# Forty-eight adaLN modulation tiles as row products on VectorE instead of matmuls on TensorE, in the first mixer of a two-layer backbone

## Chip, cores and metric

One core of one Trainium2 chip runs the whole program. The metric is the device time of one execution in microseconds (us), the median of three runs. Engines are called TensorE (PE, its weight loads PEld), VectorE (DVE), ScalarE (ACT), GpSimd (POOL) and SyncE (SP, whose queue issues nearly all DMAs).

## What is computed

Two layers over 256 context and 256 latent tokens of width 1024. Each layer has a token mixer with four branches (gated linear attention, Hyena convolution, HGRN2, differential attention), merged by gates and projected, and then a mixture of 16 experts. Both halves are modulated by vectors that come from the conditioning vectors `c` (latents) and `c_ctx` (context):

```
sc, scc = silu(c), silu(c_ctx)
for l in range(DEPTH):
    mod_x = split(sc  @ ada_w[l] + ada_b[l], 6)
    mod_c = split(scc @ ada_w[l] + ada_b[l], 6)
    h  = rms_norm(x) * (1 + mod[1]) + mod[0]
    x  = x + mod[2] * mixer(h)
    h2 = rms_norm(x) * (1 + mod[4]) + mod[3]
    x  = x + mod[5] * experts(h2)
```

`ada_w[l]` is 1024 x 6144 in float32, so one of its six chunks is 4 MB. Only two vectors are multiplied with it, so nearly all of the work is bringing it in.

## The kernel before

The tokens lie along the free dimension, the 1024 channels over 128 partitions in 8 blocks. `mixer(l, ...)` goes through the blocks of the input projection one by one. `load(name)` brings a block of weights (128 x 1024, 512 KB) by a DMA on SP, ScalarE rounds it to a high part (L798), and VectorE forms the low part by a subtraction (L799). `col_block` then runs 24 matmuls of 512 columns over 8 blocks of channels (high times high, high times low, low times high) into the PSUM tile `pd`. Around these blocks stand: the filters of the Hyena branch for both layers (`hyena_filters`, L692 to L730), the scan of the gated linear attention (`scan`, L878 to L977, tiles `ps`), two HGRN2 units with a scan each (`hg_unit`), the norms and rotations of the attention's q and k (`group_rsqrt` L654, L1144 to L1152), the attention, and `merge`, which takes 8 blocks of gates for each of the four branches (L852, L860, L864). The Hyena branch itself runs between the second and the third merge.

The modulation of layer 0 for chunks 2 to 5 and of layer 1 for chunks 1 and 0, 48 tiles of 512 KB in all, runs in the background of the first mixer. `AdaBack.run(n)` is called with a credit after each level of a scan, each query block, each block of weights. A step (`Ada.step`, L466) brings a tile of 128 rows and 1024 columns of `ada_w` into one of two buffers and runs four matmuls with 32 stationary columns (two of them are the vectors) into the PSUM tile `pa`, each on its own 32 columns of the array. After the eighth tile of a chunk, `mod_write` copies the sum (L446), transposes it on TensorE (L425, tile `pm`), and adds the bias into `mod[l]` (L453, twice). Layer 1's chunks 2 to 5 come later, at the end of the first experts, in the same way.

The order in which instructions stand on each engine is not that of the code. A scheduler gives each instruction a priority by its place in the code, and lets an engine take work from further on when nothing earlier is ready by its own reckoning. The engines then run their queues strictly in order. The numbers behind a tile's name in order listings count tiles; `base` is the large SBUF area, `r` with a number one of the areas that change type with the phase.

Of the kernel before, what the change touches and what calls it, by code (L numbers as in the profile page):

```python
# [13 lines left out]
AF = mybir.ActivationFunctionType  # L14
# [3 lines left out]
D = 1024  # L18
# [5 lines left out]
RA, RB = 12288, 12288                            # columns of the two regions that change type with the phase  # L24
BASE = 52736 - RA - RB
ENGS = ('AV', 'AVG')                             # engines of the copies of q and k, by layer
# steps of the modulation (by layer, of which parts may be left over) among the other work
TR = (0, 2, 0.5)                                 # at the end of the experts, before and among the second mixer's h
SCN = (0.5, 0.5)                                 # per level of a scan
FL = (1, 1)                                      # the rest before the merge  # L30
DAS = (0.5, 1)                                   # per head and query block
ADA = (2, 2)                                     # per block of w_in
FIRST = ("gk", "gq")                             # blocks of the second mixer loaded during the experts
AHEAD = ((0, 0), (0, 5))                         # tiles of experts loaded during the mixers


# ---------------------------------------------------------------- layouts
# [21 lines left out]
LATE = CN.at["adab"][0]                          # those from here on give way to weights of the experts  # L59
C0 = Pack()                                      # needed at the start only  # L60
# [104 lines left out]
def dft():  # L165
    """Transforms at the odd frequencies 2 pi (k + 1/2) / 512, k < 256, where no wrapped term meets the 511 of the
    convolution. Phases are counted from the middles of the signal, 127.5, of the filter's tap 128, and of the
    outputs 128..383; cosines are then even and sines odd in t <-> 255 - t, and half of the t will do."""
# [10 lines left out]
def pack_inputs(a):  # L179
    """Layout of the inputs; every element is a copy of an input's element or a constant of the shapes."""  # L180
# [50 lines left out]
    for l in range(2):  # L231
# [5 lines left out]
        wb = a["w_branch"][l].reshape(4, 2, 128, 2, 4, 128)          # i, k, p, half, d, n  # L237
        for i in range(4):
            for h in range(2):
                wg[l, BIDX[f"wb{i}{h}"]] = wb[i, :, :, h].transpose(1, 2, 0, 3).reshape(128, 8, 128)   # p, (d, k), n  # L240
# [4 lines left out]
    o["wa"] = wa.reshape(2, 128, KB * 32)  # L245
    for n in ("ada_w", "moe_w1", "moe_w3", "moe_w2"):
        o[n] = np.ascontiguousarray(a[n])
# [3 lines left out]
# ---------------------------------------------------------------- device  # L251
class Mem:
    """Columns of one SBUF tile, those longest free first; Tile sees which bytes each instruction touches."""
# [7 lines left out]
    def take(self, n, avoid=None):  # L261
        """avoid: first and last + 1 of columns not to be touched."""
# [39 lines left out]
    def merge(self):  # L302
        """Joins neighbouring free runs (their stamps become the latest)."""
        out = []
        for o, c, t in self.free:
            if out and out[-1][0] + out[-1][1] == o:
                o0, c0, t0 = out.pop()
                o, c, t = o0, c0 + c, max(t, t0)
            out.append((o, c, t))
        self.free = out  # L310

    def cut(self, b, n):
        """Gives the first n columns of b back; the rest stays."""
# [12 lines left out]
class Buf:  # L326
# [3 lines left out]
    def __call__(self, off=0, dims=None, p0=0, np_=128, n=None):  # L330
        """AP of rows p0..p0+np_, from column off, free dims [[stride, count], ...]."""
# [19 lines left out]
def build(tc, ins, outT, dbg=None, stop=None):  # L351
# [30 lines left out]
    # ---------------- persistent  # L382
    cn = mem.take(CN.n)
    sm = mem.take(SM.n)                              # of the layer
    cs_b = mem.take(256)
    mod = [mem.take(96) for _ in range(2)]          # [6 chunk, 8 k, 2 stream]
    xb = [mem.take(4096), 0]                         # [stream, k, 256]; columns cut off in front
    x_at = xb[0].at
    NR = 3
    raws = [mem.take(1024) for _ in range(NR)]       # blocks of the mixers' weights as they come  # L390
# [45 lines left out]
    # ---------------- adaLN  # L436
    def load_c(c):
        """silu(c) of both streams, 32 columns for each block of 128."""
# [17 lines left out]
    class Ada:  # L456
        """Streams ada_w[l] in tiles of one k-block of a 1024-column chunk."""
# [17 lines left out]
    class AdaBack:  # L475
        """The same in the background, in two buffers of its own."""
# [6 lines left out]
        def run(self, n=None):  # L483
            """n: steps, or parts of one."""
# [12 lines left out]
    # ---------------- little helpers  # L497
    def rsqrt_small(x, n, y, t):
        """y = x ** -0.5 on n columns (x, y, t: functions of nothing giving APs)."""
# [6 lines left out]
    def rms_rows(l, t0, mem=mem, nsq=3):  # L506
        """1/rms over d of x, on every partition: PSUM [128, 512 - t0]."""
# [26 lines left out]
    class TokenSums:  # L534
        """Sums over d while x comes block by block: x^2, and x against a [d, 16] matrix per stream."""
# [17 lines left out]
        def tokens(self, mem):  # L553
            """PSUM [token, [tb, s] of x^2 | 64: [tb, s, 16]]."""
# [17 lines left out]
    def rs_tokens(p, ns, mem):  # L572
        """1/rms: Buf whose columns 8.. are [tb, s]."""
# [6 lines left out]
    def bcast_rs(s, ns):  # L580
        """PSUM [128, (s, t)]: 1/rms on every partition."""
# [157 lines left out]
    def mixer(l, last, ada_bg, rm, sums):  # L739
# [518 lines left out]
        if FL[l]:  # L1258
            ada_bg.run()
# [506 lines left out]
```

## Time and profile before

| | before |
|---|---|
| median of 3 runs | 2050.81 us (2050.77 to 2059.14) |
| span of the profiled execution | 2046.6 us, 4.2 us under the median |
| PE busy | 1883.5 us, 92% |
| DVE busy | 801.6 us, 39% |
| ACT busy | 525.8 us, 26% |
| HBM read | 544.03 MB, 267 GB/s over the span |

The span runs from the first to the last instruction of the one execution that the profiler took; the runs' times include what lies around it. A matmul's end is modelled, so a busy PE is one that has matmuls under way. In the trace a float32 matmul stands as two records, so the four matmuls of a modulation tile are eight records.

### The profile page before, as it was taken

The numbers are of one execution on the slowest core, as the hardware profiler recorded it, in microseconds if no ns is written. First come the engines' busy times: TensorE is split into PE (matmuls) and PEld (weight loads), VectorE is DVE, ScalarE is ACT, GpSimd is POOL, SyncE is SP. The second block draws the span as 40 slices with busy tenths as digits, with TensorE's granted clock in tenths as the row PEclk, the third lists the DMA queues.
The fourth block names the chain that finished last, engine by engine and source line by source line (L and its number), as shares of the span: only waits on it lengthen the run. The fifth ranks groups of instructions, "written<-read, shape, count | busy, mean of one in ns | idle before, by whom it ended". The sixth has DMA issues, their size and how long they took to land.

```text
span 2046.6 us, 28476 instructions
## 1 busy us (share of the span) xinstructions
PE 1883.5 (92%) x11722; PEld 1091.5 (53%) x11722; DVE 801.6 (39%) x1768; ACT 525.8 (26%) x929; POOL 27.4 (1%) x52
## 2 busy tenths in 40 slices
PE   7999999999999799999887899999998999997877
PEld 3666677887886434434232356888996433231213
DVE  5455648747442323212120245769864111010101
ACT  4433336622231211101000243447442100000000
POOL 0000000000000000000000010001000000000000
PEclk9989999999999899999999999999999999999999
DMA  7734521222335799999999855324577999999999
GB/s 306 231 128 145 185 95 63 93 92 74 134 121 219 293 388 386 351 409 409 409 409 409 320 201 194 106 95 143 196 257 287 388 409 409 409 409 409 409 409 331
DMA packets 154005, 549.03 MB, mean 268 GB/s; under 512 B 11026, under 2 KB 22674, under 8 KB 153108
## 3 DMA queue, kind: packets, MB, share of 16 engines
q1 hardware_dynamic: 153300, 544.08, 70.3%
q0 software_dynamic: 576, 3.15, 0.4%
q8 instruction: 92, 1.51, 0.3%
q14 instruction: 37, 0.30, 0.0%
HBM read 544.03 MB, written 3.15 MB: 267 GB/s over the span
## 4 chain that ended last, share of the span: by engine, by line
PE 72%; DMA 18%; DVE 5%; issue 3%; ACT 2%; SPq 0%; DVEq 0%; ACTq 0%
PE pd L428 42%; PE ps L428 15%; DMA r<-moe_w 8%; PE pm L428 7%; DMA base<-moe_w 6%; PE pa L428 6%; DMA base<-ada_w 2%; PE pm L425 2%; DMA base<-wg 1%; PE ps L1591 1%; ACT r L798 1%; DVE r L799 1%; DMA base<-xT 0%; PE ps L425 0%; DVE r L1189 0%
## 5 line engine op out<-in xcount | busy, mean ns | idle before, releaser
L428 PE MATMUL pd<-r 128*128 128x256 f32 (+3 forms) x2976 | 582.8, 365 | 11.2 <-DMA r<-moe_w 6.7
L428 PEld LDWEIGHTS pd<-r 128*128 128x128 f32 (+2 forms) x2976 | 424.9, 184 | 146.1 <-issue 73.1
L428 PE MATMUL pd<-r,r 128*128 128x512 f32 (+3 forms) x1304 | 282.5, 433 | 12.1 <-DMA r<-moe_w 9.4
L799 DVE TENSOR_TENSOR r<-base,r 128x1024 fp32r<-128x1024 f32 x136 | 165.8, 1221 | 159.7 <-ACT r L798 156.5
L428 PEld LDWEIGHTS pd<-r,r 128*128 128x128 f32 (+2 forms) x1304 | 161.8, 166 | 107.0 <-issue 58.3
L798 ACT ACTIVATE r<-base 128x1024 fp32r<-128x1024 f32 x136 | 143.3, 1058 | 283.1 <-PE pd L428 224.2
L428 PE MATMUL ps<-base 32*64 32x64 f32 (+12 forms) x2372 | 176.7, 278 | 13.2 <-DMA base<-hy 4.8
L428 PE MATMUL pd<-r,base 128*32 128x512 f32 (+1 forms) x680 | 167.8, 599 | 13.5 <-DMA r<-moe_w 11.5
L428 PEld LDWEIGHTS ps<-base 32*64 32x64 f32 (+7 forms) x2372 | 112.4, 142 | 74.2 <-issue 42.2
L428 PE MATMUL pm<-base 128*128 128x128 f32 (+12 forms) x660 | 112.8, 327 | 18.9 <-issue 11.6
L428 PE MATMUL ps<-r,base 128*64 128x512 f32 (+4 forms) x468 | 98.6, 525 | 13.5 <-DVE base L1592 6.3
L428 PEld LDWEIGHTS pm<-base 128*128 128x128 f32 (+5 forms) x660 | 73.8, 180 | 66.1 <-issue 38.6
L428 PE MATMUL pd<-base 128*32 128x512 f32 (+1 forms) x408 | 101.4, 596 | 6.4 <-DMA base<-moe_w 5.6
L428 PEld LDWEIGHTS pd<-r,base 128*32 128x32 f32 (+1 forms) x680 | 42.0, 122 | 113.7 <-issue 74.4
L1588 DVE TENSOR_TENSOR r<-base,pd 64x512 f32<-64x512 f32 x16 | 10.9, 680 | 212.6 <-PE pd L428 212.6
L1587 ACT ACTIVATE base<-pd 128x512 f32<-128x512 f32 (+1 forms) x32 | 19.0, 594 | 253.9 <-PE pd L428 253.9
L1588 DVE TENSOR_TENSOR base<-base,pd 128x512 f32<-128x512 f32 x16 | 11.0, 687 | 185.7 <-PE pd L428 151.5
L428 PE MATMUL pa<-r,r 128*128 128x512 f32 (+1 forms) x384 | 82.6, 342 | 1.1 <-DVE base L860 1.1
L428 PE MATMUL pa<-base 128*32 128x256 f32 (+1 forms) x704 | 74.6, 399 | 7.7 <-DMA base<-ada_w 7.5
L428 PE MATMUL pd<-base,r 128*32 128x512 f32 (+1 forms) x296 | 71.3, 597 | 9.4 <-DMA base<-moe_w 9.4
L1638 ACT ACTIVATE base<-ps 32x512 f32<-32x512 f32 (+2 forms) x28 | 14.7, 525 | 253.8 <-PE ps L428 249.4
L1638 ACT ACTIVATE r<-ps 32x512 f32<-32x512 f32 (+2 forms) x32 | 15.3, 479 | 247.6 <-PE ps L428 242.1
(241 smaller groups left out, 1636.2 us busy)
## 6 DMA issues: line engine op xcount, KB each, us to landing
r<-moe_w SPq DMA_DIRECT2D x251, 1024.0 KB, 18.1
base<-moe_w SPq DMA_DIRECT2D x131, 1024.0 KB, 17.7
base<-wg SPq DMA_DIRECT2D x152, 512.0 KB, 3.3
base<-ada_w SPq DMA_DIRECT2D x84, 512.0 KB, 4.6
r<-ada_w SPq DMA_DIRECT2D x12, 512.0 KB, 10.7
base<-xT SPq DMA_DIRECT2D x4, 1024.0 KB, 6.5
filters<-r SPq DMA_DIRECT2D x8, 256.0 KB, 4.0
base<-filters POOLq DMA_DIRECT2D x2, 1024.0 KB, 6.6
```

The lines of the kernel that those rows point to most:

```text
L425: T.transpose(out, in_, ident)
L428: return T.matmul(out, lhsT, rhs, start=start, stop=stop, **kw)
L798: A.activation(w[0](), raw(), AF.Copy)
L799: V.tensor_tensor(w[1](), raw(), F(w[0]()), op=OP.subtract)
L1587: A.activation(s_(np_=rows), pa[0:rows, :], AF.Silu)
L1588: V.tensor_tensor(h_(np_=rows), s_(np_=rows), pb[0:rows, :], op=OP.mult)
L1591: T.transpose(p[:, q * rows:q * rows + rows], h_(q * 128, n=128, np_=rows), cs("ident", n=rows, np_=rows))
L1638: A.activation(dst, src, AF.Copy)
```

## The change

The inputs get two more arrays: `ada_t`, `ada_w` with the columns of a chunk's 128-column block as rows (a block is 128 x 1024, contiguous), and `cb`, the two conditioning vectors. A class `AdaRows` takes the place of `AdaBack` in the first mixer. At its start it brings `cb` to all 128 partitions and applies SiLU in one ScalarE instruction. A step brings one block of `ada_t` into one of two buffers, and for each of the two vectors runs one `tensor_tensor_reduce` on VectorE: product of the block with the vector, sum along the row, started at the bias, into one column of `mod[l]`. The products themselves go to a scratch tile, or for the second vector over the block. Credits in layer 0 are now given only once `merging` is set: 1.25 for each block of weights, the rest before the output projection. The matmuls, `mod_write` and the PSUM tile `pa` of these 48 tiles fall away. The second layer's modulation stays as it was, and so do the first 16 tiles.

```diff
-SCN = (0.5, 0.5)
-FL = (1, 1)
-DAS = (0.5, 1)
-ADA = (2, 2)
+SCN = (0, 0.5)
+FL = (0, 1)
+DAS = (0, 1)
+ADA = (0, 2)
+ADM = (1.25, 2)
...
+    o["ada_t"] = np.ascontiguousarray(a["ada_w"].reshape(2, D, 48, 128).transpose(0, 2, 3, 1))
+    o["cb"] = np.stack([a["c_ctx"], a["c"][0]])
...
+    class AdaRows:
+        def __init__(self, todo):
+            self.todo = [(l, c, j) for l, c in todo for j in range(8)]
+            self.buf = mem.take(5120)
+            self.raw, self.junk, self.cb = [view(self.buf, 1024 * i, 1024) for i in range(2)], view(self.buf, 2048, 1024), view(self.buf, 3072, 2048)
+            src = ins["cb"]
+            S.dma_start(out=self.cb(n=2048), in_=bass.AP(tensor=src.tensor, offset=src.offset, ap=[[0, 128], [1, 2048]]))
+            A.activation(self.cb(n=2048), self.cb(n=2048), AF.Silu)
+            self.left, self.credit, self.n = len(self.todo), 0, 0
+
+        def run(self, n=None):
+            self.credit = self.left if n is None else self.credit + n
+            while self.credit >= 1 and self.left:
+                l, c, j = self.todo.pop(0)
+                b = self.raw[self.n % 2]
+                S.dma_start(out=b(), in_=ins["ada_t"][l, c * 8 + j])
+                for s in range(2):
+                    V.tensor_tensor_reduce(self.junk() if s == 0 else b(), b(), self.cb(s * 1024, n=1024), 1.0,
+                                           cs("adab", l * 48 + c * 8 + j, n=1), OP.mult, OP.add,
+                                           mod[l](c * 16 + j * 2 + s, n=1))
+                self.n += 1
+                self.left -= 1
+                self.credit -= 1
+                if not self.left:
+                    self.buf.free()
...
-            ada_bg.run(ADA[l])
+            ada_bg.run((ADM if merging[0] else ADA)[l])
...
-                p = ps("s" if ada_bg.left else "a")
+                p = ps("s" if l and ada_bg.left else "a")
...
+        merging[0] = True
         merge(0, True)
         merge(2, False)
-        ada_bg.run()
+        if l:
+            ada_bg.run()
...
         merge(3, False)
         merge(1, False)
+        ada_bg.run()
...
-                ada = AdaBack([(0, c) for c in range(2, 6)] + [(1, 1), (1, 0)], mem.take(2048))
+                ada = AdaRows([(0, c) for c in range(2, 6)] + [(1, 1), (1, 0)])
```

Lines of the changed program lie about 31 further down in the mixer: L799 becomes L830, L917 L948, L935 to L939 L966 to L970, L860 L891, L654 L685, L1144 L1175. The product stands in listings as `L519 ISA`, two instructions: the product over 1024 columns, and the reading of its sum, 128x1.

On VectorE, at the filters of layer 1's Hyena branch (L723 to L731 now), the order before has the chain of small steps alone:

```order
79 L692 TENSOR_SCALAR r_530<-ps_604,base 64x256
80 L799 TENSOR_TENSOR r_227<-base,r_227 128x1024
81 L693 TENSOR_SCALAR r_530<-r_530 64x256
82 L694 TENSOR_SCALAR r_530<-r_530 64x256
83 L699 SCALAR_TENSOR_TENSOR r_530<-r_530 64x256 x3
84 L700 TENSOR_SCALAR r_530<-r_530 64x256
85 L692 TENSOR_SCALAR r_530<-ps_614,base 64x256
```

The same place in the changed program:

```order
104 L730 SCALAR_TENSOR_TENSOR r_485<-r_485 64x256
105 L519 ISA base<-base 128x1024
106 L519 ISA base 128x1
107 L730 SCALAR_TENSOR_TENSOR r_485<-r_485 64x256
108 L519 ISA base<-base 128x1024
109 L519 ISA base 128x1
110 L730 SCALAR_TENSOR_TENSOR r_485<-r_485 64x256
```

The products now stand between the links of the chain. They are not in the merge: the first of the 96 is row 67 of VectorE's order, the last row 511, and the first gate step of a merge (L891) is row 533. Ten stand before the chain above, 35 from there to the end of the first scan, 38 in the two HGRN2 units, 13 in the norms and rotations of the attention's q and k.

On TensorE, in the first scan (the 64x64 matmuls on tiles `ps`), the order before puts blocks of weights (`pd`) and modulation tiles (`pa`, 32x256) between the heads:

```order
99 L428 MATMUL ps_771<-base 64x64 x8
100 L428 MATMUL ps_781<-base 64x64 x8
101 L428 MATMUL ps_791<-base 64x64 x8
102 L428 MATMUL ps_801<-base 64x64 x8
103 L428 MATMUL pa_1231<-base 32x256 x3
104 L428 MATMUL pd_1241<-r_227 128x512 x8
105 L428 MATMUL ps_815<-base 64x64 x8
```

Now 31 such tiles of the scan follow each other with nothing between them; these are the last of them:

```order
85 L431 MATMUL ps_932<-base 64x64 x8
86 L431 MATMUL ps_947<-base 64x64 x8
87 L431 MATMUL ps_958<-base 64x64 x8
88 L431 MATMUL ps_969<-base 64x64 x8
89 L431 MATMUL pd_1138<-r_227 128x512 x3
90 L431 MATMUL ps_980<-base 64x64 x8
91 L431 MATMUL pd_1138<-r_227 128x512 x14
```

Of the 52 block matmuls that stood among those of the first scan, 17 now come at its very end and some 28 after it, between the first scan and the second.

## Rows read from the trace of the kernel before

**Rows 1.** The page: engines, and the chain that ended last by engine.
```profile
PE 1883.5 (92%) x11722; PEld 1091.5 (53%) x11722; DVE 801.6 (39%) x1768; ACT 525.8 (26%) x929; POOL 27.4 (1%) x52
PE 72%; DMA 18%; DVE 5%; issue 3%; ACT 2%; SPq 0%; DVEq 0%; ACTq 0%
```

**Rows 2.** Stretches: length, then PE, PEld, DVE, ACT, POOL busy, PEclk, DMA share, GB/s.
```profile
55.40:87.30 31.90, 31.65 (x216) 23.15 (x217) 9.47 (x17) 20.25 (x27) 0.31 (x1) 1.00 0.69 232
87.30:161.20 73.90, 69.80 (x834) 47.37 (x828) 42.30 (x88) 22.86 (x40) 2.17 (x4) 0.91 0.47 151
161.20:294.60 133.40, 130.20 (x1290) 92.90 (x1290) 63.50 (x127) 43.95 (x79) 3.44 (x5) 1.00 0.43 144
294.60:318.40 23.80, 22.68 (x107) 17.27 (x108) 19.70 (x51) 11.86 (x17) 0.00 (x0) 1.00 0.27 90
400.00:680.00 280.00, 279.64 (x1218) 210.51 (x1217) 131.38 (x192) 75.55 (x103) 0.00 (x0) 1.00 0.36 129
```

**Rows 3.** Timeline: start, duration, engine, line; a modulation tile on PE and its neighbours.
```profile
91.32 0.64 PE L428 MATMUL pa<-base 128*32 128x256 f32 x8 [0.20 <-DMA base<-ada_w]
91.89 2.14 PE L428 MATMUL pd<-r,r 128*128 128x512 f32 x8
```

**Rows 4.** Waits from 60 to 320 us: who for what, us, times, longest.
```profile
PEld pa L428 <- DMA base<-ada_w: 8.7, 11, 1.7
PE pa L428 <- DMA base<-ada_w: 5.0, 6, 1.5
```

**Rows 5.** Timeline of VectorE: two 128x1024 products of two tensors, one step between.
```profile
52.72 1.22 DVE L799 TENSOR_TENSOR r<-base,r 128x1024 fp32r<-128x1024 f32 x1
53.85 0.41 DVE L778 TENSOR_TENSOR r<-base,r 128x256 fp32r<-128x256 f32 x1
54.19 1.22 DVE L799 TENSOR_TENSOR r<-base,r 128x1024 fp32r<-128x1024 f32 x1
```

**Rows 6.** VectorE's groups by shape, 0 to 700 us: count, busy us, mean ns, idle.
```profile
L1204 DVE TENSOR_SCALAR base<-base 128x1 f32<-128x1 f32 x32 | 4.2, 145 | 0.1
L1210 DVE SCALAR_TENSOR_TENSOR base<-base 128x512 f32<-128x512 f32 x8 | 6.0, 746 | 0.1
L446 DVE COPY base<-pa 128x256 f32<-128x256 f32 x8 | 3.4, 419 | 4.6 <-PE pa L428 4.5
L453 DVE TENSOR_TENSOR base<-pm,base 128x8 f32<-128x8 f32 x16 | 2.0, 157 | 0.6 <-PE pm L425 0.5
```

**Rows 7.** Timeline of VectorE: one level of the first scan and the next one's start.
```profile
139.44 1.68 DVE L917 COPY_PREDICATED base<-base,ps 128x256 f32<-128x256 int32 x4
141.02 0.67 DVE L937 TENSOR_TENSOR base<-base 128x512 f32<-128x512 f32 x1
141.73 0.19 DVE L939 TENSOR_TENSOR base<-base 128x32 f32<-128x32 f32 x1
142.02 0.69 DVE L935 TENSOR_TENSOR base<-base 128x512 f32<-128x512 f32 x1
142.86 1.67 DVE L917 COPY_PREDICATED base<-base,ps 128x256 f32<-128x256 int32 x4
```

**Rows 8.** ScalarE's groups by shape, 0 to 700 us, columns as in rows 6.
```profile
L798 ACT ACTIVATE r<-base 128x1024 fp32r<-128x1024 f32 x68 | 71.7, 1058 | 207.8 <-PE pd L428 185.6 <-issue 17.3 <-DMA base<-wg 4.7
L709 ACT ACT_TABLE_LOAD x3 | 3.8, 1283 | 0.1
```

**Rows 9.** The chain in order of time (start, us): two blocks of a merge.
```profile
436.48 5.50 PE pd L428 x24
443.37 5.50 PE pd L428 x24
```

**Rows 10.** The tile query on ada_w: its transfers from issue to landing.
```profile
DMA to landing us min/median/max: 3.3/4.7/12.7
```

**Rows 11.** Stretches at the end of the filters, columns as in rows 2.
```profile
100.00:105.00 5.00, 3.50 (x24) 1.50 (x23) 1.38 (x2) 1.26 (x2) 0.00 (x0) 0.95 0.79 270
105.00:110.00 5.00, 5.00 (x26) 4.16 (x19) 0.37 (x2) 1.06 (x1) 0.00 (x0) 0.50 0.39 128
```

More of the change, by code (lines that the diff above doesn't have):

```diff
@@ L787, in mixer @@
         dump(f"hh{l}", F(hh()))
-        ri, wi = [0], [0]
+        ri, wi, merging = [0], [0], [False]
         def load(name):
@@ L1746, in build @@
     big.__exit__(None, None, None)
-_KEYS = ("xT", "cn", "c0", "df", "sm", "hy", "hyr", "wg", "wa", "ada_w", "moe_w1", "moe_w3", "moe_w2")
+_KEYS = ("xT", "cn", "c0", "df", "sm", "hy", "hyr", "wg", "wa", "ada_w", "ada_t", "cb", "moe_w1", "moe_w3", "moe_w2")
 def kernel(**inputs):
```

## The prediction, made before the changed kernel had run

> **What bounds the kernel now.** The page comes first [rows 1]: TensorE is busy for 92% of the span, VectorE for 39%, and the chain that ended last is TensorE for 72%. So TensorE's work looks worth saving and VectorE's time free. But these are averages over a program of many stages, and what counts is the stage in which the new work stands. By the order of the changed program, all 96 products stand ahead of the first gate step, at places that the trace of before passes between 55 and 318 us. I cut that time into four stretches at landmarks that both orders share [rows 2]: A, the first blocks (55.4 to 87.3); B, the filters of layer 1 and the first scan (to 161.2); C, the two HGRN2 units (to 294.6); D, the norms and rotations of q and k (to 318.4). The fifth row is for the merges. The reader should see that TensorE is busy nearly throughout A to D, while VectorE's share is 30% in A, 57% in B, 48% in C and 83% in D. In B and D VectorE is already half a bound. The timeline of one scan level says it more sharply [rows 7]: from one group of masked copies to the next, 139.44 to 142.86, VectorE has no gap over 0.2 us, and TensorE must wait for these copies to get its PSUM tiles back.
>
> **What is removed.** A modulation tile is eight records on TensorE, and the next block's matmul starts 0.57 us after the tile's first [rows 3]. 48 tiles are 27.4 us: 1.1 ahead of A, then 8 tiles (4.6 us) in A, 12 (6.8) in B, 26 (14.8) in C. The tiles also made TensorE wait for their transfers: 8.7 us at the weight loads, which overlaps the 5.0 us at the matmuls [rows 4]. VectorE loses six writes of a chunk, 0.42 + 2 x 0.16 = 0.73 us each [rows 6]: one in A, one in B, four in C.
>
> **What is added.** No row shows the new instruction. Its nearest row is the product of two 128x1024 tensors: 1.22 us from end to end, 1.13 us from its start to the next instruction's [rows 5]. The reading of the sum is a 128x1 instruction, and the nearest on VectorE takes 0.145 us [rows 6]. Lower end: the reading is hidden, 1.13 us in all. Upper end, where the reading must wait for the product to finish: 1.22 + 0.145 = 1.37 us. I take 1.25, the middle, since a following product can overlap at least the reading. 96 x 1.25 = 120 us.
>
> [...] The row first: VectorE's three-operand step on two float32 sources in SBUF takes 746 ns for 512 columns [rows 6], about the rate of the plain product, but it writes out no sum. [...]
>
> **The sum, stretch by stretch.** Products by the new order: 10 in A, 35 in B, 38 in C, 13 in D.
>
> - A: VectorE 9.5 - 0.7 + 12.5 = 21.3 us of 31.9, so the products are hidden behind TensorE. TensorE saves 4.6 us. ScalarE gets a SiLU over 2048 columns, 2 x 1.06 us, and a table load of 1.28 [rows 8], ahead of the first weights; most of these 3.4 us falls beside the slower VectorE, I charge 1. Net -4.
> - B: VectorE 42.3 - 0.7 + 43.8 = 85.4 us, where the stretch had 73.9. VectorE becomes the bound: +11.5. The order confirms it, for the products stand between the links of the filters' chain and one in each scan level, and TensorE's blocks no longer fill the scan. A buffer is refilled only after its second product: two products and one landing, 2.5 + 4.7 us [rows 10], for two tiles, so 3.6 us a tile where products follow each other, against 2.5. The five products just ahead of the scan are such a run: 2.5 tiles x 1.1 = 3 us. Net +14.5.
> - C: VectorE 63.5 - 2.9 + 47.5 = 108.1 of 133.4 us. TensorE saves 14.8 us and about half of the waits, 4, and gets 28 block matmuls out of B, at 5.50 / 24 = 0.23 us each [rows 9] 6.4 us. That would be -12; but runs of 9, 5 and 12 products with their transfers stand in VectorE's queue ahead of the steps of the units, whatever waits behind them, so I take half: -6.
> - D: VectorE 19.7 + 16.3 = 36.0 us where the stretch had 23.8: +12. In its queue the steps of the norms and also the low parts of the merge's next weights (L830) stand behind products, so TensorE's own fill there is late too.
> - After D nothing is moved. The merges have VectorE busy for 131 of 280 us [rows 2], and there the 120 us would have fitted; but the products don't stand there. In layer 1 nothing changes.
>
> Sum: -4 + 14.5 - 6 + 12 = +16.5 us. The span of the profiled execution is 2046.6 and the median 2050.8, 4.2 apart, which I carry over: **2067 us**, 0.8% slower. With a product at 1.13 us, B and D give 35 x 0.12 + 13 x 0.12 = 5.8 less, and without the 3 us of landing 2058; at 1.37 us 5.8 more, and if all 24 tiles of B and D waited 1.1 us for their transfer, 23 more: 2096. Below nothing is possible too; that is the first rival.
>
> One thing I leave at nothing: TensorE's clock. [...]
>
> **The rivals.**
>
> 1. *VectorE packs perfectly (faster).* Over A to D VectorE has 135 - 4.4 us of old work; with 120 us of products 251, with 1.13 us each 239. The four stretches last 263 us, and TensorE's own work shrinks by 26 us and 8.7 of waits to 228. So if the idle 25 us of VectorE in C could take up what is too much in B and D, the time would be 239 to 251: 12 to 24 us less, 2027 to 2039. It decides at the order: products that overflow B must delay nothing on TensorE. For it: the scheduler did move TensorE's blocks around. Against it: both queues are in order, and the masked copies that TensorE waits for stand behind products. Chance 0.18.
> 2. *The two cancel.* The cost of B and D is half of what I count, because TensorE has blocks ahead in its queue while it lasts, and A and C give their full 4 + 12: within 10 us of 2051. Chance 0.27.
> [...]
>
> That the change doesn't do what it says needs no chance of its own: the products do stand in the filters, scans and norms and not in the merge, and the sum is made with that.
>
> **How the numbers follow.** The forecast, slower by 10 to 45 us with its own range 2058 to 2096, has 0.48. About 0.5%, 10 us, is what a measurement of this kernel can tell from no change. Slower by more: 0.48 + 0.07 = 0.55; the same 0.27; faster 0.18. The range 2030 to 2098 leaves out the half rate (0.07), the lower end of the first rival (0.05) and a little above (0.03).
>
> **What would show it.** A product row on VectorE of 1.1 to 1.25 us with a reading of 0.1 to 0.2; VectorE over 90% busy from the filters to the end of the first scan, which should last about 88 us; TensorE with 20 to 30 us of idle or of waits for VectorE there (on L948's copies above all); the norms of q and k about 12 us longer; no modulation work in the merges, with the same 6.9 us from block to block [rows 9]. I am wrong if the first scan ends no later than before, or if a product takes over 1.5 us. If TensorE's waits name the transfer of `ada_t`, the landing term was the larger.

## The result, and the profile after

The changed kernel takes 2070.6 us (median of 4 runs, 2067.55 to 2075.62), the kernel before 2050.8 beside it (4 runs, 2041.57 to 2059.14): a ratio of 1.0103, 95% interval 1.0074 to 1.0133. It is 1.0% slower; 2067 had been forecast. The profiled execution has a span of 2068.5 us, 21.9 over that of before.

The page of the changed kernel, engines and the chain that ended last, against [rows 1]:

```profile
PE 1868.5 (90%) x11326; PEld 1096.6 (53%) x11326; DVE 910.7 (44%) x1942; ACT 530.3 (26%) x931; POOL 26.3 (1%) x52
PE 70%; DMA 18%; DVE 6%; issue 3%; ACT 2%; SPq 1%; DVEq 0%; ACTq 0%
```

The two groups of the new line, from VectorE's groups by shape, columns as in [rows 6]:

```profile
L519 DVE CUSTOM_DVE_ANT_0 base<-base 128x1024 f32<-128x1024 f32 x96 | 122.4, 1279 | 12.0 <-DMA base<-ada_t 11.3
L519 DVE DVE_READ_ACCUMULATOR2_ANT base<- 128x1 f32 x96 | 7.9, 82 | 0.0
```

TensorE has 15 us less work and the span is 22 longer: nothing on the page but VectorE's 109 us more could say where, and an average over the span does not. So the two traces are laid side by side at instructions that both have. The lag is the time in the changed kernel less the time before:

| landmark | before | after | lag | step |
|---|---|---|---|---|
| first step of layer 1's filters (L692, now L723) | 87.36 | 83.83 | -3.5 | A -3.5 |
| first product of the first scan (L935, L966) | 124.15 | 133.38 | +9.2 | B +12.8 |
| first product of the second scan | 161.27 | 181.26 | +20.0 | B +10.8 |
| first norm of q and k (L654, L685) | 294.62 | 295.75 | +1.1 | C -18.9 |
| a gate of the first merge (L860, L891) | 444.02 | 460.81 | +16.8 | D and attention +15.7 |
| in the experts, near 690 | 689 | 706 | +16.8 | merges 0.0 |

After the merges, where both kernels run the same code, the lag drifts to 21.9. Every kernel below drifts by 3 to 10 us there against this one profile of before, whose span lies 4 us under the median of its runs (2 us of that is what a run's time has around its span, 2070.3 to 2068.5 in the changed kernel), so I read nothing into it.

The stretches of [rows 2], cut at the landmarks of the changed kernel, same columns; the last row is the merges':

```profile
55.40:83.80 28.40, 28.40 (x161) 22.55 (x156) 21.35 (x32) 19.89 (x29) 0.31 (x1) 0.98 0.66 219
83.80:181.30 97.50, 69.59 (x728) 51.41 (x730) 82.43 (x157) 26.82 (x48) 2.11 (x5) 0.68 0.42 137
181.30:295.70 114.40, 113.20 (x1076) 89.26 (x1072) 106.58 (x192) 43.84 (x74) 2.42 (x4) 1.00 0.42 140
295.70:334.50 38.80, 28.56 (x124) 21.47 (x125) 36.97 (x82) 10.83 (x15) 0.00 (x0) 0.85 0.49 161
400.00:680.00 280.00, 279.93 (x1228) 213.57 (x1228) 138.82 (x208) 80.59 (x114) 1.23 (x2) 1.00 0.37 130
```

B is now 97.5 us with TensorE busy for 69.6 of them at a clock of 0.68 (0.91 before), though it has 12 tiles less to do. C has TensorE busy for all but a microsecond. D has VectorE busy for 37.0 of 38.8 us.

**In the filters** the chain of waits alternates between links of the filters' chain and pairs of a product and its reading (line, pieces; start and length in us):

```profile
99.98 1.20 DVE base L519 x2
101.18 0.20 DVE r L725
101.39 1.20 DVE base L519 x2
102.59 0.03 DVE r L730
102.62 3.96 DMA base<-ada_t
```

A link of 0.20 us is followed by 1.20 us of product. The 3.96 us are the transfer from its issue to its landing, not idle time: VectorE has two more products and two links beside it and then waits for 0.59 us (timeline):

```profile
106.60 1.28 DVE L519 CUSTOM_DVE_ANT_0 base<-base 128x1024 f32<-128x1024 f32 x1 [0.59 <-DMA base<-ada_t]
```

Five products stand between the links from 98.1 to 107.8 us, and TensorE waits for the sine at the chain's end.

**In the scan** one level on VectorE, to be held against [rows 7] (timeline):

```profile
145.47 0.68 DVE L968 TENSOR_TENSOR base<-base 128x512 f32<-128x512 f32 x1
...
146.81 1.28 DVE L519 CUSTOM_DVE_ANT_0 base<-base 128x1024 f32<-128x1024 f32 x1
148.02 0.08 DVE L519 DVE_READ_ACCUMULATOR2_ANT base<- 128x1 f32 x1
148.02 1.10 DVE L948 COPY_PREDICATED base<-base,ps 128x256 f32<-128x256 int32 x3
...
150.01 0.68 DVE L968 TENSOR_TENSOR base<-base 128x512 f32<-128x512 f32 x1
```

From 145.47 to 150.01 is 4.54 us, where a level before took 3.42, and there is one product in it. The product's successor starts 1.21 us after it, with the reading inside that time. But the product is only half of the difference. In hold_merge below, which has no product here, TensorE's timeline shows a level every 4.0 us:

```profile
125.49 2.77 PE L431 MATMUL ps<-base 32*64 32x64 f32 x64 [1.22 <-DVE base L975]
129.47 2.79 PE L431 MATMUL ps<-base 32*64 32x64 f32 x64 [1.22 <-DVE base L975]
```

And the same levels in the kernel before:

```profile
138.71 1.91 PE L428 MATMUL ps<-base 32*64 32x64 f32 x64
140.55 1.65 PE L428 MATMUL pd<-r 128*128 128x512 f32 x6
142.14 1.91 PE L428 MATMUL ps<-base 32*64 32x64 f32 x64
```

There blocks fill TensorE while VectorE works, at a granted clock of 1.00 (140 to 150 us). Without them TensorE waits 1.22 us a level for VectorE, and at a clock of 0.50 (130 to 140 us in hold_merge) its own 64 matmuls take 2.8 us and not 1.9.

**At the end of D** VectorE's timeline shows the worst single place:

```profile
325.10 1.28 DVE L519 CUSTOM_DVE_ANT_0 base<-base 128x1024 f32<-128x1024 f32 x1
...
327.63 0.76 DVE L696 COPY base<-base 128x512 f32<-128x512 f32 x2
329.27 1.28 DVE L519 CUSTOM_DVE_ANT_0 base<-base 128x1024 f32<-128x1024 f32 x1 [0.88 <-DMA base<-ada_t]
...
330.48 0.74 DVE L1175 SCALAR_TENSOR_TENSOR base<-base,pm 128x512 f32<-128x512 f32 x1
```

Four products stand ahead of the copies (L696) for which TensorE waits 7.4 us, and a fifth ahead of q's norm (L1175). For that one's block, given back at 325.1 us and landed 4.1 us later, VectorE itself waits 0.88 us. What TensorE waits for in the whole of A to D (who for what, us, times, longest), where before it waited 5.0 us for `ada_w` and 3.4 for VectorE's steps:

```profile
PE ps L431 <- ACT r L732: 12.9, 2, 11.8
PE ps L431 <- DVE base L968: 9.4, 8, 2.0
PE pm L428 <- DVE base L696: 7.4, 1, 7.4
PE pm L431 <- DVE base L1175: 2.8, 2, 2.0
```

The first is the end of the filters' chain (the sine), the second the scan, the next two the norms. For the copies L948, which the prediction named above all, it waits 1.7 us. In the merges the chain of waits is as in [rows 9]:

```profile
432.51 5.50 PE pd L431 x24
...
439.40 5.50 PE pd L431 x24
```

### The profile page after: what moved, and what is told of

Same layout as the page of the kernel before. It is cut to its first block, busy times and chain, and to the rows that moved or that the text cites. A ratio compares the mean times of both kernels' runs of the same rounds, so it can differ in the third digit from the quotient of the medians.

```text
span 2068.5 us, 27867 instructions
## 1 busy us (share of the span) xinstructions
PE 1868.5 (90%) x11326; PEld 1096.6 (53%) x11326; DVE 910.7 (44%) x1942; ACT 530.3 (26%) x931; POOL 26.3 (1%) x52
## 4 chain that ended last, share of the span: by engine, by line
PE 70%; DMA 18%; DVE 6%; issue 3%; ACT 2%; SPq 1%; DVEq 0%; ACTq 0%
PE pd L431 41%; PE ps L431 15%; DMA r<-moe_w 11%; PE pm L431 7%; PE pa L431 5%; DMA base<-moe_w 4%; DMA base<-ada_w 1%; PE pm L428 1%; DVE base L519 1%; DMA base<-wg 1%; DMA base<-ada_t 1%; DVE r L830 1%; PE ps L1625 1%; ACT r L829 1%; DMA base<-xT 0%
## 5 line engine op out<-in xcount | busy, mean ns | idle before, releaser
L830 DVE TENSOR_TENSOR r<-base,r 128x1024 fp32r<-128x1024 f32 x136 | 166.1, 1222 | 116.7 <-ACT r L829 113.5
L431 PE MATMUL ps<-base 32*64 32x64 f32 (+12 forms) x2372 | 181.7, 291 | 23.5 <-DVE base L968 9.4
L431 PEld LDWEIGHTS ps<-base 32*64 32x64 f32 (+7 forms) x2372 | 118.6, 156 | 82.1 <-issue 45.4
L431 PE MATMUL pm<-base 128*128 128x128 f32 (+12 forms) x660 | 117.1, 332 | 21.8 <-issue 11.6
L519 DVE CUSTOM_DVE_ANT_0 base<-base 128x1024 f32<-128x1024 f32 x96 | 122.4, 1279 | 12.0 <-DMA base<-ada_t 11.3
L1622 DVE TENSOR_TENSOR r<-base,pd 64x512 f32<-64x512 f32 x16 | 10.9, 679 | 213.8 <-PE pd L431 213.8
## 6 DMA issues: line engine op xcount, KB each, us to landing
r<-ada_w SPq DMA_DIRECT2D x12, 512.0 KB, 10.6
```

Of the source, the lines that this page charges most:

```text
L431: return T.matmul(out, lhsT, rhs, start=start, stop=stop, **kw)
L519: V.tensor_tensor_reduce(self.junk() if s == 0 else b(), b(), self.cb(s * 1024, n=1024), 1.0, cs("adab", l * 48 + c * 8 + j, n=1), OP.mult ...
L830: V.tensor_tensor(w[1](), raw(), F(w[0]()), op=OP.subtract)
L1622: V.tensor_tensor(h_(np_=rows), s_(np_=rows), pb[0:rows, :], op=OP.mult)
```

## The experiments

My theory after the result: products cost where VectorE is the bound (B and D), and would cost nothing in the merges. Rivals: the transfers of `ada_t` with their two buffers are the cost; TensorE's 27 us were not worth anything; the clock is. Each ratio is to the kernel before on the same chip in the same session (whose median there was between 2051 and 2058), with its 95% interval; the lag is that of the table above.

**no_products: transfers without products.**

```
-                    V.tensor_tensor_reduce(self.junk() if s == 0 else b(), b(), ...
+                    V.tensor_copy(mod[l](c * 16 + j * 2 + s, n=1), b(s, n=1))
```

> The 96 products and readings (L519) are left out; two 128x1 copies on VectorE (about 0.15 us each by the rows of other 128x1 steps) take the first columns of each block of ada_t instead, so the modulation is not computed; every transfer, the SiLU and all else stay. It prices VectorE's products as they stand, with the transfers kept. Theory (the products in VectorE's queue are the cost, 2.4 us a tile, and TensorE's 48 tiles are a real saving of 27 us plus some of its 5.0 us of waits): under the kernel before by 20 to 35 us, 2016 to 2031. Rival 1 (the transfers of ada_t with two buffers, and the order that the scheduler chose, are the cost): no faster than before, 2045 to 2070. Rival 2 (TensorE's saved 27 us were idle anyway in the stretches that VectorE or chains bind): 2035 to 2048.

Measured: 2041.6 us, 0.9953 (0.9932 to 0.9974). Only 10 us under the kernel before, in the range of rival 2. What VectorE waited for longest between 55 and 335 us:

```profile
DVE base L519 <- DMA base<-ada_t: 36.9, 22, 4.4
```

The copies are 0.14 us long, so little lies beside a landing any more: a copy frees the buffer, the next transfer takes 3.5 to 4.6 us behind the first scan, and the next copy waits for it with the scan's steps behind. So this kernel does not price the products alone. But these waits are hardly on the path: hold_merge below, with neither products nor copies ahead of the merges, has a lag of -13.6 us at the norms, this kernel -11.9.

**no_mod: nothing of the 48 tiles at all.**

```
-            self.buf = mem.take(5120)
...
+            for l, c in todo:
+                V.memset(mod[l](c * 16, n=16), 0.0)
+            self.left = 0
```

> The 48 tiles are left out altogether (no products, no transfers of ada_t, no SiLU; the vectors are set to zero), so the modulation is not computed: the price of what no_products kept. Theory (the transfers cost little themselves; what the tiles cost TensorE is real only outside the filters and the first scan): 2032 to 2041, little under no_products (2041.6). Rival (the transfers, and the copies that wait for them, take what TensorE saved): 2015 to 2030, near the full 27 us and the waits.

Measured: 2020.8 us, 0.9822 (0.9787 to 0.9857), which is 36.5 us under the kernel before (29 to 44). My theory's range falls and the rival's holds. That fits TensorE's saving being whole (27.4 us of tiles and the 8.7 of [rows 4] are 36.1), though an interval of 29 to 44 can't show it to the microsecond. By the lag it comes at the landmarks as -4.8, -5.9 (first product of the second scan), -30.2 and -30.8 in the merges. Against this kernel the changed one adds not 20 us but 20 + 36 = 56 us (by the lag in the merges, 47.6), beside 116 us of products. They are not all the products': hold_merge and paced below have none ahead of the merges and stay some 16 us behind no_mod there. Nor is the rival's mechanism shown: beyond the first two or three transfers of `ada_t`, neither of the two has the copies or the transfers there.

**three_bufs: a third buffer.**

```
-            self.buf = mem.take(5120)
+            self.buf = mem.take(6144)
...
-                b = self.raw[self.n % 2]
+                b = self.raw[self.n % 3]
```

> Three buffers for the blocks of ada_t in place of two; nothing else is changed. Theory (the price of the products in B and D is the cost, the landing of ada_t a small term): the waits for landing, 11.3 us in all and 3.5 and 4.1 of them on the path, go for the most part: 2060 to 2067. Rival 1 (landing is the larger term, since a late product makes the whole queue late): 2045 to 2055. Rival 2 (VectorE's own work fills what landing leaves): 2067 to 2073, no difference.

Measured: 2058.8 us, 1.0030 (1.0007 to 1.0053), 12 us under the changed kernel, between the theory's range and the first rival's. The waits for `ada_t`, 11.3 us in A to D, are gone from VectorE's list. But the scheduler also moved the products. Records of line L519 (two for a product) between the landmarks of B, C and D, first the changed kernel, then this one (length, VectorE's time in them, TensorE's clock, DMA share, GB/s):

```profile
83.80:181.30 97.50, 44.97 (x72) 0.68 0.42 137
181.30:295.70 114.40, 48.63 (x75) 1.00 0.42 140
295.70:334.50 38.80, 16.88 (x28) 0.85 0.49 161
```

```profile
83.10:187.75 104.65, 56.26 (x90) 0.67 0.47 147
187.75:298.10 110.35, 50.76 (x80) 1.00 0.48 148
298.10:334.50 36.40, 1.29 (x2) 1.00 0.44 145
```

With one product in D in place of 13 the lag goes from +3.5 ahead of D to +2.6 in the merges: D's 15.7 us are gone, and they were the products in D with their landing. In B, with 44 products (counted by their starts) instead of 35 and no wait for landing (5.3 us of VectorE's waits in B in the changed kernel), the lag grows by 30.8 instead of 23.5. Nine products are 10.9 us and the step grew by 7.3. If a product in B cost its length, the landing would have cost some 4 us; one step can't tell the two apart.

**hold_scan1: products held until the first scan is over.** A step passes 0 times the scan's output into the conditioning vectors, so that no product can run before it.

```
+        def hold(self, ap):
+            z = mem.take(1)
+            V.tensor_scalar(z(), ap, 0.0, None, op0=OP.mult)
+            A.activation(self.cb(n=2048), self.cb(n=2048), AF.Identity, bias=z())
...
         gla_o = scan(32, KP, QP, q0, KP, 2.0, T1, gv, 0)
+        if l == 0:
+            ada_bg.hold(gla_o[-1][0](0, n=1))
```

> The products are held until the end of the first scan, in the same way: none stands any more in the filters and the first scan (stretch B), they spread over the HGRN2 units, the norms, the attention and the merges. Theory (B and the norms are where they cost, 23.5 us and 12 to 16 by the traces): B goes back to about 70 us, later stretches get what B had but spread over more of them: 2035 to 2055, 15 to 35 us under the changed kernel. Rival 1 (the total on VectorE is what counts, wherever it stands): 2065 to 2075. Rival 2 (the products that leave B crowd the HGRN2 scans, which VectorE binds as well): C grows by 20 us or more against the changed kernel, 2065 to 2080.

Measured: 2058.4 us, 1.0033 (1.0012 to 1.0054), 12 us under the changed kernel and 3 over the theory's range. Where they stand counts, against rival 1. The lag is -6.0 at the first scan's first product, -7.7 at the norms, and +8.8 in the merges: what was won ahead of the norms is paid in the norms and the attention.

**hold_merge: held until the attention's output is split.** The same step, ahead of the first merge.

```
+        if l == 0:
+            ada_bg.hold(F(ob[3]((2 * NB // 2 - 1) * W, n=1)))
         merging[0] = True
```

> All 96 products are held until the attention's output is split: the conditioning vectors are passed once more through ScalarE with a bias of 0 times that output. By the new order the products then stand in the merges, two to four between the steps of a gate, where VectorE was busy for 131 of 280 us in the kernel before. Theory (the place is the cost: VectorE was the bound in the filters, the first scan and the norms): 149 us of idle take up 96 x 1.21 = 116 us, TensorE keeps its saving of 27 us and most of 5 us of waits, less some 5 us at the weights' low parts that stand behind products: 2020 to 2030, faster than both kernels. Rival (96 products are too much in front of the steps that TensorE waits for anywhere, L830 and L891 in the merges): 6.9 us a block grows to 7.5 or more over 38 blocks, 23 us, 2045 to 2070.

Measured: 2074.4 us, 1.0117 (1.0071 to 1.0163): slower than the kernel before, my theory's range missed by 44 us. The lag says where: -10.6 us at the gate at 444, +21.1 at the one at 521. From the chain of waits there:

```profile
445.57 4.59 DMA base<-ada_t
...
450.18 1.29 DVE base L526 x2
451.48 1.14 DVE r L837
452.61 1.22 DVE base L526 x2
...
453.85 4.43 DMA base<-ada_t
```

This is a loop of 8.3 us in place of 6.9 a block: product, freed buffer, transfer, product, and the low part of the next weights (L837) behind it. The weights' own transfer stands behind that of `ada_t` in SP's queue. From 440 to 500 us these are waits of VectorE and of TensorE:

```profile
DVE base L526 <- DMA base<-ada_t: 3.1, 5, 0.8
PE pd L431 <- DVE r L837: 8.4, 5, 2.4
```

So the landing is a small part: of each 8.3 us VectorE is busy for 7.5, with four products, and TensorE waits for the low parts behind them. SP issued two of `ada_t` for each of the weights here: the scheduler brought the tiles forward, where 48 tiles over 38 blocks are 1.25.

**hold_3b and hold_gq: two ways out of that loop.** One has a third buffer, the other issues `ada_t` from GpSimd's queue.

```
-            self.buf = mem.take(5120)
+            self.buf = mem.take(6144)
...
-                b = self.raw[self.n % 2]
+                b = self.raw[self.n % 3]
```

> Products held until the merges (as hold_merge) with three buffers in place of two. In hold_merge the chain of waits from 440 to 500 us goes product, landing of ada_t (4.3 us), product, low part of the weights (L837), and the weights' transfer stands behind that of ada_t in SP's queue. Theory (the loop of two products, freed buffer, landing is what lengthened the blocks there by some 30 us): with a third buffer the landing lies beside two products, and most of the loss goes: 2035 to 2050. Rival (the products in front of the gate steps on VectorE are what lengthened them): 2065 to 2080.

```
-                S.dma_start(out=b(), in_=ins["ada_t"][l, c * 8 + j])
+                G.dma_start(out=b(), in_=ins["ada_t"][l, c * 8 + j])
```

> Products held until the merges (as hold_merge) with two buffers, but the transfers of ada_t issued from GpSimd's queue in place of SP's. Theory A (what costs is that the weights' transfers stand behind those of ada_t in SP's queue, whose issue waits for a product): the weights come in time, 2035 to 2050. Theory B (the products wait for their landing in VectorE's queue, with the weights' low parts behind them, whichever queue issues): no better than hold_merge, 2065 to 2080.

Measured: hold_3b 2066.2 us, 1.0069 (1.0049 to 1.0089); hold_gq 2079.6, 1.0130 (1.0090 to 1.0170). Which queue issues made no difference that is shown (1.0130 beside 1.0117 of hold_merge, with intervals that overlap): theory B of hold_gq. The third buffer takes the landing off the chain, and the time is 8 us less, though the intervals of hold_merge and hold_3b just overlap; it is the rival's range, for the products are next. From the chain of waits of hold_3b:

```profile
421.52 0.60 DVE base L898
422.12 2.41 DVE base L526 x4
424.53 0.60 DVE base L902
425.13 2.41 DVE base L526 x4
```

Two products stand behind every step of a gate. VectorE is busy without a gap from 400 to 460 us, and TensorE is at 13.6 to 16.8 of each 20 us.

**paced: one and a quarter tiles a gate, forced by data.** The bias that starts a sum is passed through GpSimd with 0 times the gate just formed.

```
+                if ap is not None:
+                    bc = self.bias(self.n % 8, n=1)
+                    G.tensor_scalar(bc, ap, 0.0, bias, op0=OP.mult, op1=OP.add)
+                    bias = bc
...
                 V.scalar_tensor_tensor(g(), g(), 1.0, p[:, 0:W], op0=OP.add, op1=OP.mult)
+                if l == 0:
+                    ada_bg.run(1.25, g(0, n=1))
```

> Products paced by data: each tile's bias passes through a 128x1 step on GpSimd that adds 0 times the gate just formed (1.25 tiles after each of the 32 gates and the 6 blocks of the Hyena branch), so that the scheduler can't bring tiles forward; three buffers. Theory (in hold_3b VectorE had four products after every step of a gate, 100% busy from 400 to 460 us, and TensorE waited for the low parts of the weights behind them; at 1.25 tiles, 3.0 us, beside about 3.3 us of other work per 6.9 us it has room): the 14 us that hold_merge had ahead of the merges stay, 2030 to 2042. Rival (any product in front of L837 and L898's steps costs TensorE its length): 38 blocks by 0.5 to 1 us, 2055 to 2080.

Measured: 2066.6 us, 1.0051 (1.0035 to 1.0068), in the rival's range, but not by the rival's way: 38 blocks did not each get longer. The lag is about -15 at 320 us, +3.7 from 420 to 460, between 11 and 23 at 520, 15.3 from 540 and 14.5 at 640. Blocks of the first merge stand among the attention, and with their products the lag grows by 18 us there; in the Hyena branch it grows by some 11 more; the regular blocks, 410 to 460 and 540 to 640 us, take nothing.

**np_fill: is it the clock?** In the first scan of no_products the granted clock is 0.50 from 130 to 145 us. Eight matmuls that nobody reads are put into each level.

```
                 ada_bg.run(SCN[l])
+                if l == 0 and dk == 32:
+                    pf, fr = ps("a"), kl if 0 <= lev < 6 else q0
+                    for j in range(8):
+                        mm(pf[32 * (j % 4):32 * (j % 4) + 32, 0:256], cs_b(0, n=32), fr(256 * (j % 2), n=256), True, True)
```

> The kernel without products (no_products; the modulation is not computed), and in each level of the first scan eight more matmuls of 32 columns by 256 on TensorE that nobody reads: 72 in all, by the tile's price (four of them 0.57 us) 10 us of added work at the upper clock. Theory (the modulation tiles had kept TensorE's clock at its upper level in the first scan: without them the granted clock there is 0.50 for some 25 us, and the blocks that follow run at half speed): the scan's stretch returns to a clock of 0.9 or more and gets shorter although work is added, 2031 to 2039 against 2041.6 without. Rival (TensorE's saved time is not on the path in the scan, and the clock costs nothing there because VectorE sets the pace): the added matmuls cost up to their time or nothing, 2041 to 2052.

Measured: 2038.1 us, 0.9929 (0.9909 to 0.9949), against 0.9953 (0.9932 to 0.9974) without: the intervals overlap, so no difference is shown. The clock did return in part (1.00 from 140 to 150 us, 0.50 still from 130 to 140), but from the scan's first product to its last copies (L928) took 36.0 us against 33.6. The added 10 us of work cost little or nothing in all, but clock and added work can't be told apart by this run, since the new matmuls stand between the scan's levels themselves. That the clock costs something there is seen in the levels of hold_merge above, 2.8 us at 0.50 in place of 1.9 at 1.00.

**mixed, mixed2, mixed3: a version that beats both.** The first leaves 16 tiles as matmuls in the filters and scans and paces 32 by the gates, the Hyena blocks included.

```
-                ada = AdaRows([(0, c) for c in range(2, 6)] + [(1, 1), (1, 0)])
+                ada = AdaMix([(0, 2), (0, 3)], [(0, 4), (0, 5), (1, 1), (1, 0)])
...
+                if l == 0:
+                    ada_bg.run(1.0, g(0, n=1))
```

> 16 of the 48 tiles stay matmuls on TensorE and stand in the filters and the first scans, as in the kernel before; the other 32 go by rows, paced as in paced, one tile after each gate or Hyena block, three buffers. Theory (the tiles in the first scan cost little, since they keep TensorE's clock up and fill its waits; what is worth moving are the 26 tiles of the HGRN2 units and what VectorE has room for in the merges): 2025 to 2036, at least as fast as paced though TensorE has 9 us more of work. Rival (a tile on TensorE costs its 0.57 us anywhere): 5 to 9 us slower than paced.

Measured: 2056.2 us, 1.0010 (0.9991 to 1.0029), no difference from before and 10 us faster than paced: its rival is refuted, its theory's size as well. The lag is -18 at 340 us and +0.9 at the gate at 437: lost in the attention and the first merge's blocks again. So mixed2 allows no product before the attention's output, none behind the first merge's gates and none in the Hyena branch, and mixed3 has 24 tiles each way and one tile a gate.

```
-            A.activation(self.cb(n=2048), self.cb(n=2048), AF.Silu)
+            A.activation(self.cb(n=2048), self.cb(n=2048), AF.Silu, bias=z())
...
+                if l == 0 and br:
+                    ada_bg.run(1.34, g(0, n=1))
...
+        if l == 0:
+            ada_bg.begin(F(ob[3](3 * W, n=1)))
         merging[0] = True
```

> As mixed (16 tiles as matmuls in the filters and scans, 32 by rows), but no product before the attention's output is split (SiLU of the conditioning vectors is formed there, with a bias of 0 times that output), none after the gates of the first merge and none in the Hyena branch: 1.34 tiles after each of the 24 gates of merges 2, 3 and 1. Theory (mixed was 18 us ahead of the kernel before at 340 us and lost 19 in the attention, where VectorE is over 85% busy as well; in the regular merges paced lost nothing from 410 to 460 and from 540 to 640 us): 2030 to 2042, faster than both kernels. Rival (VectorE's products cost TensorE something beside every gate): 2045 to 2060.

> As mixed2 with 24 tiles as matmuls and 24 by rows, one tile after each of the 24 gates. By TensorE's price for eight more tiles 4.6 us slower than mixed2 (2035 to 2047) if the gates of mixed2 take 1.34 tiles at no cost; 2 to 8 us faster than mixed2 if a third of a tile more per gate is what fills VectorE (2.9 + 3.3 of 6.9 us by the rows of before's merges, against 2.9 + 2.4).

Measured: mixed2 2038.5 us, 0.9927 (0.9912 to 0.9942); mixed3 2037.3, 0.9919 (0.9903 to 0.9934). Both are faster than the kernel before by 15 to 17 us and than the changed one by 32 to 33; between them nothing is shown. Two stretches of mixed3 with regular blocks of the merges, and beneath them those of the kernel before (columns as in [rows 2]):

```profile
408.00:480.00 72.00, 72.00 (x316) 57.35 (x315) 51.42 (x74) 21.62 (x28) 3.71 (x5) 1.00 0.44 145
530.00:650.00 120.00, 120.00 (x495) 86.94 (x494) 74.25 (x106) 32.23 (x42) 7.46 (x11) 1.00 0.57 202
```

```profile
408.00:480.00 72.00, 72.00 (x315) 58.68 (x314) 34.63 (x46) 19.93 (x25) 0.00 (x0) 1.00 0.28 95
530.00:650.00 120.00, 120.00 (x517) 89.93 (x516) 46.18 (x64) 32.82 (x43) 0.00 (x0) 1.00 0.46 172
```

VectorE takes 17 us more in 72 and 28 more in 120, and TensorE has no gap in either. The lag of mixed3 is -11.1 us at 440 and -11.2 at 640, of mixed2 -16.5 at both: here 24 and 32 tiles cost nothing.

## Why the prediction held

The total is right, and the reason in part: the products do not stand where VectorE has room, and they cost their time in the filters and the norms. At the merges the lag is +16.8 us where the steps summed to +16.5, but so close a sum is luck: B came out 9.0 us larger than said, C 12.9 better, D 3.7 larger. In the scan the reason was another than the one given.

- *The products' price*: 1.25 us was taken, 1.21 from one product's start to the next instruction's is measured; the reading (0.08 us) is hidden. No run shows a product at half rate, for which the chances set 0.07 aside: the 96 products over 1024 columns, with two float32 sources in SBUF and a sum, took 1.28 us in the mean, next to 1.22 for the plain product [rows 5].
- *The places*: 10, 35, 38 and 13 products start in A to D, as read from the order; of the 35 in B, 23 before the scan's first product. None stands in the merges.
- *A*: -4 said, -3.5 measured.
- *B*: +14.5 said, +23.5 measured. VectorE's work there, 82.4 us, is what was summed (85.4), but it is busy for 85% of the stretch and not over 90: the step "VectorE becomes the bound: +11.5" took its work to be without gaps. VectorE has 15.1 us of gaps: it waits 5.3 us for `ada_t`, where 3 were charged, and most of the rest for TensorE, because the links of both chains go from one engine to the other. Nor is it the bound all along. hold_merge, without a product ahead of the merges, is at -7.1 us at the scan's first product and at -13.6 at the norms, the changed kernel at +9.2 and +1.1. By this comparison the 23 products of the filters cost 16.3 us, but from there to the norms both gain about the same (6.5 and 8.1 us), and the 50 products in between are not what costs there. no_mod gains 22.7 us in that stretch. In it 78 block matmuls (tile `pd`) stand from the first scan's first product to the second scan's, 56 in the kernel before, 26 in hold_merge and 24 in the changed kernel; TensorE waits 1.1 us between 116 and 175 us in no_mod and 9.5 in hold_merge. The prediction saw that "TensorE's blocks no longer fill the scan", but gave that no price, left the clock at nothing, and took VectorE to be the bound. In the scan that was not all: TensorE's own matmuls, at a granted clock of 0.50 (140 to 165 us), are 2.8 to 3.3 us of each level of 4.5, and of the blocks that follow the scan, at 164.6 us, 14 matmuls took 5.69 us at a clock of 0.56 (165 to 170 us), where 24 take 5.50 [rows 9] at 1.00 (436 to 450 us in the kernel before), some 2.5 us.
- *C*: -6 said, -18.9 measured. The saving of 14.8 us and of 4 us of waits came whole: the tiles' records in C take TensorE 18.5 us before and 0.7 now, each counted to the next record's start. The 28 block matmuls came too (`pd` has 415 records in C where it had 381, and 71 in B where it had 100), but 31 records of the second scan's own matmuls (`ps`) went from C to B, and the two about cancel (+3.4 and -4.1 us). The half that was taken off for the runs of products is what failed: TensorE idles for 1.2 us in C.
- *D*: +12 said, +15.7 measured to the merges. VectorE is busy for 37.0 us (36.0 summed) and has 1.8 us of gaps, 1.2 of them for `ada_t`, where none were counted; the clock there is 0.85 in place of 1.00. In three_bufs, with one product in D, nothing of it is left.
- *The landing term*: VectorE waits for `ada_t` 11.3 us in A to D, 3.5 of them just ahead of the scan, in the run of products that was named. TensorE's waits name VectorE and ScalarE, not `ada_t`.
- *The rivals*: VectorE does not pack (rival 1); in B and D nothing is halved (rival 2). "There the 120 us would have fitted" was half true: hold_merge, hold_3b and paced show that only the regular blocks of the merges have room, at 1 to 1.34 tiles a gate, not 48 tiles at any pace.

What stays open: kernels without any product ahead of the merges (hold_merge, paced) have a lag of -14 to -15 us there, no_mod -30.8. The traces show where these 16 us arise, between the first scan's first product (-7.1, -7.6 and -7.5) and the norms (-13.6, -13.4 and -30.2), and what differs on TensorE there, the blocks among the scan's levels. Why the scheduler places them so is not shown: the buffers that stay allocated meanwhile, the first transfers and the step that holds are what differs in the programs, and none was tried alone.

## What to carry to other kernels

Work moved to an engine with a low share of the span is worth what the engine's busy time is in the very stretch where the instructions stand (VectorE had 39% of the span before, and 83% of D); read that place from the order of the queues, because a scheduler that thinks an engine idle brings the work forward past the place in the code. If a place must hold, hold it by data, and pace it: a buffer that is freed by the work itself makes a loop of work and landing, in which everything behind it in the queue takes part (8.3 us a block in hold_merge, 6.9 before). And before pricing such a change by leaving a part of it out, look at what the order of the other engines becomes: every kernel here is ordered anew by the scheduler, and the first scan's levels were longer without products too (4.0 us in hold_merge, 3.4 before), where TensorE's blocks had left them.

## What the runs showed that I had not expected

- The product with a sum over 128x1024 float32 from two SBUF sources takes 1.28 us, its reading 0.08, and the next instruction starts 1.21 us after the product's start, inside the reading.
- TensorE's granted clock was 0.50 to 0.55 in the stretches of B and D where the filters, the scan or the norms left it gaps: 0.55 from 95 to 125 us (busy for 13.6 of 30), 0.51 from 135 to 165 (21.1 of 30) and 0.50 from 325 to 340 (7.5 of 15) in the changed kernel. In the first two of these the kernel before, whose blocks and tiles stood there, had 0.83 (27.3 of 30) and 1.00 (29.5 of 30). Filling the scan with matmuls that nobody reads (np_fill) brought nothing that can be measured (0.9929 beside 0.9953).
- Two short copies per transferred block (no_products) cost nearly 27 us more than no block at all (0.9953 against 0.9822), although SP's 12 transfers of `ada_t` in a row, from 142 to 169 us, are not the reason for most of it: hold_merge, with no transfers there, is only 2 us further ahead in the merges (-13.8 against -11.8 at 421 us).
